# GLA decode passes, decode steps per column tile and the width of the weight rounding in a hybrid decoder layer

## The chip, the cores and the metric

The kernel runs on one core of a Trainium2 chip. The metric is the device time of one execution in microseconds; the median of three runs of the kernel before is 847.57 us.

## What is computed

One layer of a hybrid recurrent decoder, for a prompt of 256 tokens and for 8 sequences that decode one token each, 264 columns in all. A combined projection feeds an mLSTM branch and a gated linear attention (GLA) branch. Both keep a state per head; for a decoding sequence the GLA part is

```python
def _gla_chunk(q, k, v, loga, S):
    ...
    o = jnp.einsum('bhtd,bhde->bhte', q * jnp.exp(bc), S) + jnp.einsum('bhts,bhse->bhte', a, v)
    ...
    S_new = jnp.exp(last[:, :, 0, :])[..., None] * S + jnp.einsum('bhsd,bhse->bhde', k * jnp.exp(last - bc), v)
```

With one token this is S_new = a * S + k v and o = q S_new, for 8 sequences, 4 heads and a state of 128 x 256. The mLSTM decode has the same form with a state of 256 x 256. Each branch is normed per head, gated and projected; sigmoid gates merge the branches, an output projection and a LayerNorm follow.

## The kernel before

All large projections run as 128 column tiles of 128 output columns (`units()` lists them; a 129th, small one holds gate columns). A tile takes 16 blocks of contraction rows, and for each block three products of 128 x 128 weights with 264 columns: high half of the weights with the high half of the activations (L225), high with low (L226) and low with high (L230). The halves are made on the chip: `load_raw` brings 8 blocks (512 KB) by one transfer, `cast_piece` takes 4 blocks, 512 columns wide, rounds them on ScalarE to the high half (L204) and subtracts on VectorE for the low half (L206). Four raw buffers and nine pieces of each half let this run ahead of TensorE; `LA` says how many pieces are asked for ahead in the program.

In program order a loop goes over the column tiles: ask for pieces, issue the 48 products, take the result from PSUM (`e_qk`, `e_v`, `e_plain`, `e_raw`, `e_pab`, `e_out`), then call `pump(budget)`. The rest of the layer is written as generators that yield a cost after each step: gates, mLSTM prompt (`g_a_prompt`), mLSTM decode (`g_a_decode`), GLA prompt (`g_gla_prompt`), GLA decode (`g_gla_decode`), the two norms (`g_a_norm`, `g_b_norm`). `pump` takes one step of every live generator, decode ones last, as long as the budget of the tile (4.0) is above zero. TensorE's order is the program's order; the other engines are ordered by a scheduler from priorities (the rounding has the highest, prompt and norm steps the next, decode steps none). The queue that loads (SP), POOL's and each compute engine's run strictly in their order.

The tiles come in this order: q and k of the mLSTM (tiles 0 to 15), the small one (16), its v (17 to 24), q, k, v of GLA (25 to 40), output gates of both branches (41 to 64), merge gates (65 to 96, `gr`), branch projections (97 to 112), output projection (113 to 128).

`g_gla_decode` (from L759) works on 8 chunks `sch` of 4 sequences, two per head. For a head three rows `ga`, `gk`, `gq` are flattened by a small transfer and spread over the partitions by POOL (`flatten_bcast`, L493). A chunk is multiplied by `ga` in one VectorE pass of 1024 (L784). Then each sequence and half takes an update `sch = gk * v + sch` (L788) and a dot product with `gq` that accumulates into one column (L790), each 128 wide:

```python
V.tensor_tensor(out=c, in0=c, in1=ab[:, b0:b0 + 4].unsqueeze(2).to_broadcast([128, 4, 2, 128]), op=ALU.mult)
...
V.scalar_tensor_tensor(out=cc, in0=kb[:, b, :], scalar=bvd[:, 2 * h + e, b:b + 1],
                       in1=cc, op0=ALU.mult, op1=ALU.add)
V.scalar_tensor_tensor(out=scr2[:, 0:128], in0=cc, scalar=1.0, in1=qb[:, b, :], op0=ALU.mult,
                       op1=ALU.mult, accum_out=oT.t(2 * h + e)[:, L + b:L + b + 1])
```

It yields after every two sequences (a step: 16 in all), and POOL's queue stores the finished chunk (L794). `g_b_norm` squares each head of `oT` on ScalarE (`nsq`, L803), sums on VectorE (`ns`, L805) and averages over partitions on TensorE (L810).

Of the kernel before, what the change touches and what calls it, by code (L numbers as in the profile page):

```python
# [21 lines left out]
L = 256  # L22
NB = 8
# [62 lines left out]
def body(ctx, tc, xT, wbig, wsmall, par, cmask, lmask, sel, rowc, gate, wgu, cT, sT, nst, cst, lnr,  # L86
# [34 lines left out]
    def t1(name, dt=F32):  # L121
        return tmp.tile([128, T], dt, tag="t1", name=name, bufs=12)
# [10 lines left out]
    cm_sb = const.tile([128, 384], F32, name="cm_sb")  # L133
# [33 lines left out]
    def load_raw():  # L167
        i = nxt["dma"]
        if i >= len(pieces):
            return  # L170
        r = wraw_p.tile([128, KR, 128], F32, tag="raw", name="raw")
        per = KR // KC
        runs = []
        for q in range(per):
            n, c, bi = pieces[i + q]
            w = 128 if bi is not None else SMALL
            raws[i + q] = r[:, q * KC:q * KC + KC, 0:w]
            if runs and runs[-1][0] == n and runs[-1][2] == c * KC:
                runs[-1][2] += KC
            else:  # L180
                runs.append([n, c * KC, c * KC + KC, q * KC, bi, w])
        for n, k0, k1, o, bi, w in runs:
            src = wbig[bi] if bi is not None else wsmall
            nc.sync.dma_start(out=r[:, o:o + k1 - k0, 0:w], in_=src[:, k0:k1, :])
        nxt["dma"] += per

    def cast_piece():
# [3 lines left out]
        n, c, bi = pieces[i]  # L191
        w = 128 if bi is not None else SMALL
        r = raws.pop(i)
        if bi is None:
            hl = whi_p.tile([128, KC, 128], F32R, tag="hi", name="hl")
            A.copy(out=hl[:, :, 0:w], in_=r)
            V.tensor_tensor(out=hl[:, :, w:2 * w], in0=r, in1=f(hl[:, :, 0:w]), op=ALU.subtract)
            his[n, c], los[n, c] = hl[:, :, 0:2 * w], None
            nxt["cast"] += 1
# [7 lines left out]
        his[n, c], los[n, c] = h, lo  # L207
        nxt["cast"] += 1
# [5 lines left out]
    def parts(n, k0, k1, rhs, base=0):  # L214
# [5 lines left out]
        for k in range(k0, k1):  # L220
            if k % KC == 0:
                yield ps[:, 0:T]
            wh = his[n, k // KC][:, k % KC, :]
# [1067 lines left out]
```

## Time and profile before

| | |
|---|---|
| runs | 846.61, 848.86, 847.57 us, median 847.57 |
| profiled execution | 848.32 us, of which 846.5 us lie between its first and last instruction |
| TensorE busy | 824.9 us, 97% |
| VectorE busy | 630.0 us, 74% |
| ScalarE busy | 470.6 us, 56% |
| GpSimd (POOL) busy | 82.7 us, 10% |
| mean granted TensorE clock | 0.994 |

TensorE's matmuls are pipelined, so a busy TensorE is not the same as one that advances at full pace; its waits and the number of its instructions in a stretch tell more. The other engines run one instruction after the other, and there the start of the next instruction is a better price than the shown length of one.

### The profile page before, as it was taken

To read this page: it belongs to the slowest core of one execution; us is meant where nothing else is said; L and a number is where in the kernel's file an instruction comes from. 1 tells how busy PE (TensorE), PEld (TensorE's weight loads), DVE (VectorE), ACT (ScalarE), POOL (GpSimd) and SP (SyncE) were. 2 spreads that over 40 slices of the span, in tenths; PEclk is the share of its full clock that TensorE was granted. 3 is DMA by queue.
4 is the path that set the end of the run, shared out by engine and by line. 5 is a ranking of instruction groups with operands and counts; after the bars stand their busy time and mean duration, and the time that the engine had idled before them with its cause. 6 is when DMAs were issued, how large, how long until landed. Compare 5 with 4: busy or idle time off the path is not lost.

```text
span 846.5 us, 17762 instructions
## 1 busy us (share of the span) xinstructions
PE 824.9 (97%) x6773; PEld 811.4 (96%) x6773; DVE 630.0 (74%) x1354; ACT 470.6 (56%) x896; POOL 82.7 (10%) x103
## 2 busy tenths in 40 slices
PE   6999999999999999999999999988999999999996
PEld 6999999999999999999999999988999999999995
DVE  6987768645586897876786799989895777767862
ACT  5755567545464565655655665353765444455643
POOL 0000000001010210110110202220300000000211
PEclk9999999999999999999999999999999999999998
DMA  8765565545666765676787656776656665576513
GB/s 318 243 213 178 161 188 167 155 149 166 209 211 214 259 198 188 210 232 213 238 284 227 193 164 215 256 244 216 216 170 224 185 182 178 179 260 206 179 51 103
DMA packets 50917, 170.21 MB, mean 201 GB/s; under 512 B 7936, under 2 KB 8880, under 8 KB 50832
## 3 DMA queue, kind: packets, MB, share of 16 engines
q1 hardware_dynamic: 46704, 154.66, 57.8%
q0 software_dynamic: 4128, 14.42, 4.5%
q8 instruction: 53, 0.87, 0.4%
q14 instruction: 32, 0.26, 0.1%
HBM read 152.36 MB, written 16.58 MB: 200 GB/s over the span
## 4 chain that ended last, share of the span: by engine, by line
PE 89%; DMA 4%; DVE 3%; issue 1%; ACT 1%; POOL 0%; SPq 0%; ACTq 0%; POOLq 0%; DVEq 0%
PE mm L225 27%; PE mm L226 27%; PE mm L230 27%; DMA raw<-wbig 1%; DVE lo L206 1%; DMA cch<-cT 1%; PE sd L467 1%; DVE sch L788 1%; DMA sch<-sT 1%; PE sd L423 1%; DMA sS<-sch 1%; PE sd L699 1%; DVE scr L790 1%; DMA ga<-rows 1%; PE sd L403 0%
## 5 line engine op out<-in xcount | busy, mean ns | idle before, releaser
L206 DVE TENSOR_TENSOR lo<-raw,hi 128x512 fp32r<-128x512 f32 x512 | 354.8, 702 | 137.8 <-ACT hi L204 132.9
L204 ACT CAST hi<-raw 128x512 fp32r<-128x512 f32 x512 | 310.2, 618 | 255.8 <-PE mm L226 207.3
L225 PE MATMUL mm<-xh,hi 128*128 128x264 f32 x1536 | 442.4, 288 | 8.1 <-ACT hi L204 7.4
L230 PE MATMUL mm<-xh,lo 128*128 128x264 f32 x1536 | 436.8, 284 | 4.7 <-DVE lo L206 4.7
L226 PE MATMUL mm<-xl,hi 128*128 128x264 f32 x1536 | 436.7, 284 | 0.0
L225 PEld LDWEIGHTS mm<-xh,hi 128*128 128x128 f32 x1536 | 290.7, 189 | 10.2 <-ACT hi L204 7.4
L230 PEld LDWEIGHTS mm<-xh,lo 128*128 128x128 f32 x1536 | 289.4, 188 | 5.7 <-DVE lo L206 5.6
L226 PEld LDWEIGHTS mm<-xl,hi 128*128 128x128 f32 x1536 | 291.0, 189 | 0.2
L225 PE MATMUL mm<-mh,hi 128*128 128x264 f32 x256 | 72.7, 284 | 0.0
L226 PE MATMUL mm<-ml,hi 128*128 128x264 f32 x256 | 72.6, 284 | 0.0
L230 PE MATMUL mm<-mh,lo 128*128 128x264 f32 x256 | 72.3, 283 | 0.0
L226 PEld LDWEIGHTS mm<-ml,hi 128*128 128x128 f32 x256 | 48.2, 188 | 0.0
L225 PEld LDWEIGHTS mm<-mh,hi 128*128 128x128 f32 x256 | 48.1, 188 | 0.0
L230 PEld LDWEIGHTS mm<-mh,lo 128*128 128x128 f32 x256 | 48.1, 188 | 0.0
L564 DVE SCALAR_TENSOR_TENSOR cch<-kb,avd,cch 128x256 f32<-128x256 f32 x64 | 33.1, 551 | 8.0 <-POOL kb L493 4.1
L551 ACT ACTIVATE cch<-cch,decb 128x256 f32<-128x256 f32 x64 | 28.9, 501 | 13.8 <-DMA cch<-cT 13.8
L226 PE MATMUL mm<-ybl,hi 128*128 128x264 f32 x128 | 36.5, 285 | 0.0
L226 PE MATMUL mm<-yal,hi 128*128 128x264 f32 x128 | 36.4, 284 | 0.0
L225 PE MATMUL mm<-yah,hi 128*128 128x264 f32 x128 | 36.4, 284 | 0.0
L230 PE MATMUL mm<-yah,lo 128*128 128x264 f32 x128 | 36.3, 283 | 0.0
L230 PE MATMUL mm<-ybh,lo 128*128 128x264 f32 x128 | 36.2, 283 | 0.0
L225 PE MATMUL mm<-ybh,hi 128*128 128x264 f32 x128 | 36.2, 283 | 0.0
(330 smaller groups left out, 865.5 us busy)
## 6 DMA issues: line engine op xcount, KB each, us to landing
raw<-wbig SPq DMA_DIRECT2D x252, 512.0 KB
cch<-cT SPq DMA_DIRECT2D x16, 512.0 KB
sC<-cch POOLq DMA_DIRECT2D x16, 512.0 KB, 4.7
sch<-sT SPq DMA_DIRECT2D x8, 512.0 KB
sS<-sch POOLq DMA_DIRECT2D x8, 512.0 KB, 6.7
xr<-xT SPq DMA_DIRECT2D x4, 528.0 KB
raw<-wbig SPq DMA_DIRECT2D x8, 256.0 KB
y<-yt SPq DMA_DIRECT2D x8, 256.0 KB
```

The costliest lines, as they stand in the source:

```text
L204: A.copy(out=h, in_=r)
L206: E.tensor_tensor(out=lo, in0=r, in1=f(h), op=ALU.subtract)
L225: PE.matmul(out, lhsT=wh, rhs=rh, start=(k == k0), stop=False)
L226: PE.matmul(out, lhsT=wh, rhs=rl, start=False, stop=small and k == k1 - 1)
L230: PE.matmul(out, lhsT=wl, rhs=rh, start=False, stop=(k == k1 - 1))
L423: PE.matmul(S[:, o:o + n], lhsT=kT.t(2 * h + d)[:, s0:s0 + 128], rhs=qT.t(2 * h + d)[:, t0:t0 + n], start=(d == 0), stop=(d == 1))
L467: PE.matmul(CN[:, 0:VC], lhsT=kw[:, s, d * 128:d * 128 + 128], rhs=vt[h // 2][:, s, h % 2, :], start=(s == 0), stop=(s == 1))
L551: A.activation(out=c[:, b, :], in_=c[:, b, :], func=AF.Copy, scale=decb[:, h, b0 + b:b0 + b + 1])
L564: V.scalar_tensor_tensor(out=c[:, b, :], in0=kb[:, b, :], scalar=avd[:, 2 * h + e, b0 + b:b0 + b + 1], in1=c[:, b, :], op0=ALU.mult, op1=A ...
L699: PE.matmul(pl[s0:s0 + m, 4 * hf + h, n0:n0 + w].rearrange("p (n s) -> p n s", s=hs), lhsT=K[:, h, hf * 128 + s0:hf * 128 + s0 + m], rhs=r ...
L788: V.scalar_tensor_tensor(out=cc, in0=kb[:, b, :], scalar=bvd[:, 2 * h + e, b:b + 1], in1=cc, op0=ALU.mult, op1=ALU.add)
L790: V.scalar_tensor_tensor(out=scr2[:, 0:128], in0=cc, scalar=1.0, in1=qb[:, b, :], op0=ALU.mult, op1=ALU.mult, accum_out=oT.t(2 * h + e)[:, ...
```

## The change

- GLA decode: for two sequences at a time ScalarE writes the four outer products `gk * v` of 128 columns into a new tile `gkv`; VectorE then makes three passes of 512 columns (times `ga`, plus `gkv`, times `gq` into `gpr`) and a reduce of 512 columns to four. The step yields 2.6.
- mLSTM decode: same instructions; its step of two sequences yields 2.1 instead of 1.4.
- `pump`: budget 2.8 instead of 4.0; after the other generators only the first live decode generator is stepped, up to twice, as long as the budget is above zero.
- Weights: from the third tile on, a piece has 8 blocks (1024 columns) and there are five buffers of each half; the first two tiles keep pieces of 4 blocks, interleaved as before.
- Room: 11 instead of 12 scratch tiles `t1`, a mask of 256 instead of 384 columns, and four small tiles of the last stage put into tags that are free by then.

```diff
-BUDGET = 4.0
+BUDGET = 2.8
+BACK_STEPS = 2
+T1_BUFS = 11
-KC = 4
-NC = KT // KC
 KR = 8
 RAW_BUFS = 4
-CAST_BUFS = 9
+CAST_BUFS = 5
+NC = KT // KR
 LA = CAST_BUFS - NC
-RA = (RAW_BUFS - 1) * KR // KC
+HU = 2
+KH = 4
...
-        h = whi_p.tile([128, KC, 128], F32R, tag="hi", name="hi")[:, :, 0:w]
-        lo = wlo_p.tile([128, KC, 128], F32R, tag="lo", name="lo")[:, :, 0:w]
+        h = whi_p.tile([128, KR, 128], F32R, tag="hi", name="hi")[:, 0:m]
+        lo = wlo_p.tile([128, KR, 128], F32R, tag="lo", name="lo")[:, 0:m]
         with tc.high_priority(offset=PRIO):
             A.copy(out=h, in_=r)
-            E = G if POOL_LO[0] <= n < POOL_LO[1] and c in POOL_C else V
-            E.tensor_tensor(out=lo, in0=r, in1=f(h), op=ALU.subtract)
+            V.tensor_tensor(out=lo, in0=r, in1=f(h), op=ALU.subtract)
...
-                if b == 1 and SPLIT_A:
-                    yield 1.4
-            yield 1.4 if SPLIT_A else 2.7
+                if b % 2:
+                    yield 2.1
...
-                V.tensor_tensor(out=c, in0=c, in1=ab[:, b0:b0 + 4].unsqueeze(2).to_broadcast([128, 4, 2, 128]), op=ALU.mult)
-                for b in range(b0, b0 + 4):
-                    for e in range(2):
-                        cc = c[:, b - b0, e, :]
-                        V.scalar_tensor_tensor(out=cc, in0=kb[:, b, :], scalar=bvd[:, 2 * h + e, b:b + 1],
-                                               in1=cc, op0=ALU.mult, op1=ALU.add)
-                        V.scalar_tensor_tensor(out=scr2[:, 0:128], in0=cc, scalar=1.0, in1=qb[:, b, :], op0=ALU.mult,
-                                               op1=ALU.mult, accum_out=oT.t(2 * h + e)[:, L + b:L + b + 1])
-                    if b % 2 == 1:
-                        yield 2.0
+                for p in (0, 2):
+                    q, cc, sh = slice(b0 + p, b0 + p + 2), c[:, p:p + 2], [128, 2, 2, 128]
+                    kv, pr = (tmp.tile(sh, F32, tag="t2", name=x, bufs=5) for x in ("gkv", "gpr"))
+                    for i in range(2):
+                        for e in range(2):
+                            A.activation(out=kv[:, i, e, :], in_=kb[:, b0 + p + i, :], func=AF.Copy,
+                                         scale=bvd[:, 2 * h + e, b0 + p + i:b0 + p + i + 1])
+                    V.tensor_tensor(out=cc, in0=cc, in1=ab[:, q].unsqueeze(2).to_broadcast(sh), op=ALU.mult)
+                    V.tensor_tensor(out=cc, in0=cc, in1=kv, op=ALU.add)
+                    V.tensor_tensor(out=pr, in0=cc, in1=qb[:, q].unsqueeze(2).to_broadcast(sh), op=ALU.mult)
+                    V.tensor_reduce(out=oT.h(h)[:, :, L + b0 + p:L + b0 + p + 2].rearrange("p e b -> p b e"), in_=pr,
+                                    axis=mybir.AxisListType.X, op=ALU.add)
+                    yield 2.6
...
-        for g in sorted(side, key=lambda g: g.__name__ in BACK):
-            if budget <= (BACK_MIN if g.__name__ in BACK else 0):
-                continue
...
+        for g in [g for g in side if g.__name__ not in BACK]:
+            if budget > 0:
+                with tc.high_priority(offset=SIDE_PRIO):
+                    budget -= step(g)
+        for _ in range(BACK_STEPS):
+            for g in [g for g in side if g.__name__ in BACK][:1]:
+                if budget > 0:
+                    budget -= step(g)
```

What this makes of the order is shown at three places (each row: line, operation, tile written and tiles read, shape, and how many in a row). Counted by the rounding passes ahead of them, the first and last GLA passes on VectorE stand at tiles 72 and 89 before, at tiles 64 and 80 now; the last mLSTM pass moves from tile 66 to tile 59; in program order the GLA decode ends with tile 86 before and with tile 75 now.

VectorE in the middle of the GLA decode, before (`lo` is the rounding, `scr` the dot products):
```order
L784 TENSOR_TENSOR sch<-sch,ga 128x1024
L206 TENSOR_TENSOR lo<-raw,hi 128x512
L788 SCALAR_TENSOR_TENSOR sch<-gk,bvd,sch 128x128 x4
L206 TENSOR_TENSOR lo<-raw,hi 128x512
L788 SCALAR_TENSOR_TENSOR sch<-gk,bvd,sch 128x128 x2
L206 TENSOR_TENSOR lo<-raw,hi 128x512
L788 SCALAR_TENSOR_TENSOR sch<-gk,bvd,sch 128x128 x2
L790 SCALAR_TENSOR_TENSOR scr,oT_5114<-sch,gq 128x128 x2
L206 TENSOR_TENSOR lo<-raw,hi 128x512
L790 SCALAR_TENSOR_TENSOR scr,oT_5114<-sch,gq 128x128 x3
```
and now, inside tiles 73 to 76:
```order
L786 TENSOR_TENSOR sch<-sch,gkv 128x512
L203 TENSOR_TENSOR lo<-raw,hi 128x1024
L787 TENSOR_TENSOR gpr<-sch,gq 128x512
L785 TENSOR_TENSOR sch<-sch,ga 128x512
L788 TENSOR_REDUCE oT_4723<-gpr 128x2x2
L786 TENSOR_TENSOR sch<-sch,gkv 128x512
L785 TENSOR_TENSOR sch<-sch,ga 128x512
L787 TENSOR_TENSOR gpr<-sch,gq 128x512
L785 TENSOR_TENSOR sch<-sch,ga 128x512
L788 TENSOR_REDUCE oT_4723<-gpr 128x2x2
L786 TENSOR_TENSOR sch<-sch,gkv 128x512
L785 TENSOR_TENSOR sch<-sch,ga 128x512
```
Twelve narrow instructions per step have become four wide ones, and two rounding passes stand where four stood.

ScalarE around the squares `nsq` of the GLA norm, before (`hi` is the rounding cast):
```order
L803 ACTIVATE nsq<-oT_5114 128x528
L585 COPY gr<-mm 128x264
L204 CAST hi<-raw 128x512 x4
L585 COPY gr<-mm 128x264
L204 CAST hi<-raw 128x512 x4
L585 COPY gr<-mm 128x264
L827 ACTIVATE gr<-gr 128x1056
L204 CAST hi<-raw 128x512
L803 ACTIVATE nsq<-oT_5292 128x528
L204 CAST hi<-raw 128x512 x3
L585 COPY gr<-mm 128x264
```
and now, with the last outer products `gkv`:
```order
L783 ACTIVATE gkv<-gk,bvd 128x128
L202 CAST hi<-raw 128x1024
L783 ACTIVATE gkv<-gk,bvd 128x128 x3
L202 CAST hi<-raw 128x1024
L580 COPY gr<-mm 128x264
L783 ACTIVATE gkv<-gk,bvd 128x128 x4
L202 CAST hi<-raw 128x1024
L800 ACTIVATE nsq<-oT_4723 128x528 x2
L800 ACTIVATE nsq<-oT_4895 128x528
L202 CAST hi<-raw 128x1024
L580 COPY gr<-mm 128x264
L800 ACTIVATE nsq<-oT_4895 128x528
```
The squares of the heads stood four or five tiles of casts apart; now three stand together behind the last outer products, and the fourth two rows later.

POOL's queue, before (`ISA` rows are the partition broadcasts, `sS` the stores of finished chunks):
```order
L794 DMA sS<-sch 128x1024
L493 ISA ga<-ga 128x1024
L493 ISA gk<-gk 128x1024
L493 ISA gq<-gq 128x1024
L794 DMA sS<-sch 128x1024 x3
L493 ISA ga<-ga 128x1024
L493 ISA gk<-gk 128x1024
L493 ISA gq<-gq 128x1024
L794 DMA sS<-sch 128x1024 x2
L493 ISA ga<-ga 128x1024
L493 ISA gk<-gk 128x1024
L493 ISA gq<-gq 128x1024
```
and now:
```order
L791 DMA sS<-sch 128x1024 x2
L489 ISA ga<-ga 128x1024
L489 ISA gk<-gk 128x1024
L489 ISA gq<-gq 128x1024
L791 DMA sS<-sch 128x1024
L489 ISA ga<-ga 128x1024
L489 ISA gk<-gk 128x1024
L489 ISA gq<-gq 128x1024
L791 DMA sS<-sch 128x1024 x2
L489 ISA ga<-ga 128x1024
L489 ISA gk<-gk 128x1024
L489 ISA gq<-gq 128x1024
```
The broadcasts of the second, third and fourth head now follow the stores of two, three and five chunks; before, of one, four and six.

## Rows read from the trace of the kernel before

**Rows 1.** Timeline of VectorE, 640 to 680 us: start us, us, engine, line, operation, tiles, [idle before]
```profile
651.07 0.69 DVE L206 TENSOR_TENSOR lo<-raw,hi 128x512 fp32r<-128x512 f32 x1 [0.41 <-ACT hi L204]
...
656.89 0.69 DVE L206 TENSOR_TENSOR lo<-raw,hi 128x512 fp32r<-128x512 f32 x1 [0.41 <-ACT hi L204]
```
**Rows 2.** Windows: us, busy of PE, PEld, DVE, ACT, POOL (instructions), granted clock, DMA share, GB/s
```profile
320.00:340.00 20.00, 18.68 (x221) 18.02 (x220) 13.67 (x25) 11.00 (x23) 0.00 (x0) 1.00 0.57 186
...
476.00:600.00 124.00, 118.58 (x950) 117.23 (x949) 117.92 (x305) 63.57 (x120) 22.83 (x21) 0.99 0.68 218
...
564.00:567.00 3.00, 1.77 (x15) 1.56 (x14) 2.90 (x6) 2.56 (x6) 0.17 (x2) 1.00 0.38 131
569.00:571.00 2.00, 1.07 (x9) 0.93 (x8) 1.93 (x10) 0.31 (x1) 0.40 (x1) 1.00 0.41 156
580.00:584.00 4.00, 1.41 (x11) 1.20 (x11) 2.58 (x4) 2.15 (x5) 0.00 (x0) 1.00 0.70 281
584.00:588.00 4.00, 4.00 (x23) 4.00 (x22) 4.00 (x17) 2.02 (x5) 0.00 (x0) 0.57 0.68 205
```
**Rows 3.** Waits of TensorE: engine, line, what was waited for, us in total, times, longest
```profile
PE mm L230 <- DVE lo L206: 4.7, 3, 2.6
```
**Rows 4.** Timeline of ScalarE, 470 to 600 us
```profile
562.44 0.65 ACT L803 ACTIVATE nsq<-oT 128x528 f32<-128x528 f32 x1 [3.35 <-DVE scr L790]
...
570.69 0.62 ACT L204 CAST hi<-raw 128x512 fp32r<-128x512 f32 x1 [2.87 <-DMA raw<-wbig]
...
579.16 0.65 ACT L803 ACTIVATE nsq<-oT 128x528 f32<-128x528 f32 x1 [5.95 <-DVE scr L790]
```
**Rows 5.** Timeline of VectorE in the GLA decode, no broadcast in flight
```profile
528.94 1.22 DVE L784 TENSOR_TENSOR sch<-sch,ga 128x1024 f32<-128x1024 f32 x1
530.08 1.28 DVE L206 TENSOR_TENSOR lo<-raw,hi 128x512 fp32r<-128x512 f32 x2
531.28 0.87 DVE L788 SCALAR_TENSOR_TENSOR sch<-gk,bvd,sch 128x128 f32<-128x128 f32 x3
532.07 0.68 DVE L206 TENSOR_TENSOR lo<-raw,hi 128x512 fp32r<-128x512 f32 x1
...
538.70 0.28 DVE L790 SCALAR_TENSOR_TENSOR scr<-sch,gq 128x128 f32<-128x128 f32 x1
...
539.02 0.29 DVE L790 SCALAR_TENSOR_TENSOR scr<-sch,gq 128x128 f32<-128x128 f32 x1
```
**Rows 6.** Groups of ScalarE by line and shape: count | busy us, mean ns of one | idle before
```profile
L204 ACT CAST hi<-raw 128x512 fp32r<-128x512 f32 x512 | 310.2, 618 | 255.8 <-PE mm L226 207.3 <-DMA raw<-wbig 24.1 <-ACT mh L211 7.9
L551 ACT ACTIVATE cch<-cch,decb 128x256 f32<-128x256 f32 x64 | 28.9, 501 | 13.8 <-DMA cch<-cT 13.8
L585 ACT COPY gr<-mm 128x264 f32<-128x264 f32 x32 | 11.9, 374 | 5.3 <-DVE sch L784 4.3 <-DVE sch L788 1.0
...
L827 ACT ACTIVATE gr<-gr 128x1056 f32<-128x1056 f32 x8 | 8.7, 1088 | 0.2
...
L929 ACT CAST lgh<-lgf 128x1024 fp32r<-128x1024 f32 x2 | 2.1, 1048 | 3.6 <-DMA lgf<-lnr 3.6
...
L710 ACT ACTIVATE gE<-gB 128x128 f32<-128x128 f32 x1 | 0.3, 307 | 0.0
```
**Rows 7.** Timeline of VectorE with a partition broadcast of POOL in flight
```profile
539.63 1.64 DVE L206 TENSOR_TENSOR lo<-raw,hi 128x512 fp32r<-128x512 f32 x1
541.19 1.39 DVE L805 TENSOR_TENSOR ns<-nsq 128x264 f32<-128x264 f32 x1
542.50 2.18 DVE L784 TENSOR_TENSOR sch<-sch,ga 128x1024 f32<-128x1024 f32 x1
...
565.84 0.43 DVE L805 TENSOR_TENSOR ns<-nsq 128x264 f32<-128x264 f32 x1
...
567.12 1.12 DVE L790 SCALAR_TENSOR_TENSOR scr<-sch,gq 128x128 f32<-128x128 f32 x1
...
568.28 1.12 DVE L790 SCALAR_TENSOR_TENSOR scr<-sch,gq 128x128 f32<-128x128 f32 x1
```

More of the change, by code (lines that the diff above doesn't have):

```diff
@@ L155, in f @@
         return ap.bitcast(F32)
-    pieces = []
-    idx = 0
+    pieces = [(u, k, KH, u) for k in range(0, KT, KH) for u in range(HU)]
+    idx = HU
     for n, (kind, j) in enumerate(UN):
+        if n < HU:
+            continue
         bi = None if kind == "small" else idx
         idx += kind != "small"
-        pieces += [(n, c, bi) for c in range(NC)]
-    pieces[0:2 * NC] = [pieces[u * NC + c] for c in range(NC) for u in range(2)]
+        pieces += [(n, k, KR, bi) for k in range(0, KT, KR)]
+    last = {n: i for i, (n, k, w, bi) in enumerate(pieces)}
     raws, his, los = {}, {}, {}
@@ L171, in load_raw @@
         r = wraw_p.tile([128, KR, 128], F32, tag="raw", name="raw")
[L172 to L175, printed above, removed]
+        o = 0
+        while i < len(pieces) and o + pieces[i][2] <= KR:
+            n, k, m, bi = pieces[i]
             w = 128 if bi is not None else SMALL
[L177 to L182, printed above, removed]
-            src = wbig[bi] if bi is not None else wsmall
-            nc.sync.dma_start(out=r[:, o:o + k1 - k0, 0:w], in_=src[:, k0:k1, :])
-        nxt["dma"] += per
+            src = wbig[bi] if bi is not None else wsmall
+            raws[i] = r[:, o:o + m, 0:w]
+            nc.sync.dma_start(out=raws[i], in_=src[:, k:k + m, :])
+            o += m
+            i += 1
+        nxt["dma"] = i
     def cast_piece():
@@ L190, in cast_piece @@
             load_raw()
-        n, c, bi = pieces[i]
-        w = 128 if bi is not None else SMALL
+        n, k, m, bi = pieces[i]
+        nxt["cast"] += 1
         r = raws.pop(i)
+        h = whi_p.tile([128, KR, 128], F32R, tag="hi", name="hi")[:, 0:m]
         if bi is None:
[L195 to L199, printed above, removed]
+            w = SMALL
+            A.copy(out=h[:, :, 0:w], in_=r)
+            V.tensor_tensor(out=h[:, :, w:2 * w], in0=r, in1=f(h[:, :, 0:w]), op=ALU.subtract)
+            for q in range(m):
+                his[n, k + q] = h[:, q, 0:2 * w]
             return
-        h = whi_p.tile([128, KC, 128], F32R, tag="hi", name="hi")[:, :, 0:w]
-        lo = wlo_p.tile([128, KC, 128], F32R, tag="lo", name="lo")[:, :, 0:w]
+        lo = wlo_p.tile([128, KR, 128], F32R, tag="lo", name="lo")[:, 0:m]
         with tc.high_priority(offset=PRIO):
             A.copy(out=h, in_=r)
-            E = G if POOL_LO[0] <= n < POOL_LO[1] and c in POOL_C else V
-            E.tensor_tensor(out=lo, in0=r, in1=f(h), op=ALU.subtract)
-        his[n, c], los[n, c] = h, lo
-        nxt["cast"] += 1
+            V.tensor_tensor(out=lo, in0=r, in1=f(h), op=ALU.subtract)
+        for q in range(m):
+            his[n, k + q], los[n, k + q] = h[:, q], lo[:, q]
     def split(hi, lo, src):
@@ L773, in g_gla_decode @@
         load(0)
-        scr2 = tmp.tile([128, 256], F32, tag="t1", name="scr", bufs=12)
         yield 0.1
@@ L1016, in ln_final @@
             emit(1, g)
-        sm_ = one.tile([128, 4, NB], F32, tag="lsm", name="lsm")
+        sm_ = one.tile([128, 4, NB], F32, tag="qkd", name="lsm")
         dd, d2, sv = sm_[:, 0], sm_[:, 1], sm_[:, 2]
@@ L1026, in ln_final @@
         zd = ln["zd"]
-        td = one.tile([128, 16, NB], F32, tag="td", name="td")
+        td = one.tile([128, 16, NB], F32, tag="co", name="td")
         sh = [128, 16, NB]
@@ L1084, in body @@
         V.memset(one_c, 1.0)
-        first = [parts(u, 0, 16, x_rhs) for u in range(2)]
+        first = [parts(u, 0, 16, x_rhs) for u in range(HU)]
         head = {}
@@ L1103, in body @@
             st['n'] = n
-            while nxt["cast"] < NC * (n + 1) + LA and nxt["cast"] < len(pieces):
+            while nxt["cast"] < min(last[n] + 1 + LA, len(pieces)):
                 cast_piece()
-                while nxt["dma"] < min(nxt["cast"] + RA, len(pieces)):
+                while nxt["dma"] < min(nxt["cast"] + RAW_BUFS - 1, len(pieces)):
                     load_raw()
```

90 lines of the change are left out of this document (40 added, 50 removed).

## The prediction

> **What bounds the kernel now.** I read first the windows of the engines' busy time, then the waits of TensorE, then the timelines around those waits. In the steady part TensorE sets the pace: the reader is to see two rounding passes of VectorE, four pieces apart, that is one column tile, which each wait for a cast that in turn waits for TensorE to release a buffer. They are 656.89 - 651.07 = 5.82 us apart [rows 1]. No vector or scalar work that hides under this pace is worth anything. So only the places count where TensorE does wait. They lie in one stretch, 476 to 600 us, where VectorE is busy 117.92 of 124 us [rows 2]. That is the GLA decode together with the mLSTM norm. TensorE misses 3.00 - 1.77 = 1.23 us at 564, 2.00 - 1.07 = 0.93 us at 569 and 4.00 - 1.41 = 2.59 us at 580 [rows 2]. The sum, 4.75 us, is what the table of waits puts down to the low halves of the weights, 4.7 us in 3 waits [rows 3]. [...] Together 6.45 us. One wait of 20.00 - 18.68 = 1.32 us lies earlier, at 329 us [rows 2], in the mLSTM decode. **The pool to be won is 7.8 us, under 1% of the time.**
>
> The timeline of ScalarE says how the waits come about. A square of the GLA norm stands in its queue ahead of three or four rounding casts, and waits 3.35 and 5.95 us for the last VectorE pass of its head; once a cast waits 2.87 us for its weights [rows 4]. VectorE was late, and the rounding behind it used up its lead.
>
> **The change part by part.** Starts of neighbours in the queue, not durations, give the price of a VectorE pass when it is saturated: 1024 wide with two inputs 530.08 - 528.94 = 1.14 us, 512 wide (531.28 - 530.08) / 2 = 0.60 us, a 128-wide update (532.07 - 531.28) / 3 = 0.26 us, a 128-wide dot product with its accumulator read 539.02 - 538.70 = 0.32 us [rows 5].
>
> GLA decode, per step of two sequences: before, half a 1024-wide pass, four updates, four dot products, 0.57 + 1.05 + 1.28 = 2.90 us. After, three 512-wide passes at 0.60 and one reduce. No row shows a reduce. Nearest below is the 0.26 us update (four times less data), nearest above the 1.14 us pass (twice the data); I take the 512-wide 0.60 us. So 2.40 us a step, and 16 x 0.50 = 8.0 us less on VectorE.
>
> Rounding: a tile's four passes of 0.60 become two of 1.14, 0.12 us less. On ScalarE four casts of 0.618 us become two; the nearest row is 1.048 us for a 1024-wide cast [rows 6], 0.38 us less. Outside the GLA stretch both gains lie beside TensorE's 5.82 us and cost or earn nothing; if that cover went, it would be because VectorE or ScalarE filled a tile, which outside this stretch they don't. The lead shrinks a little: five buffers leave four pieces of half a tile, 11.6 us, less one wide cast (1.05) and one wide pass (1.14), 9.5 us; before it was 11.6 - 0.6 - 0.6 = 10.4 us.
>
> The outer products: 64 new instructions of 128 columns on ScalarE. Nearest rows: 0.307 us for 128 columns with a constant scale, 0.501 us for 256 columns with a scale per row [rows 6]; I take 0.34 us, nearer to the row of the same width. With two steps in a tile ScalarE holds 2 x 1.05 + 8 x 0.34 + 0.374 for the copy out of PSUM + a quarter of the 1.088 us gate, 5.5 of 5.82 us [rows 6]. It is covered, but thinly.
>
> The order. GLA decode starts eight tiles earlier on VectorE and ends nine earlier, so the norm of its branch is done well ahead of the projection that needs it; that in itself earns nothing, as nothing waited there for long. The twelve partition broadcasts stay. Each holds VectorE up: with them in flight a rounding pass takes 1.64 us, a sum 1.39, a wide pass 2.18, each 0.96 us over its usual time (0.68, 0.43, 1.22), 2.9 us for this head; the last head shows two dot products of 1.12 us, 0.84 over their 0.28, 1.7 us [rows 5, 7]. Mean 2.3 us a head. In the changed order VectorE's work is not even: between the rounding of tile 72 and that of tile 76 stand 25 two-input passes of 512, 8 reduces and 8 wide rounding passes. That is 33 x 0.60 + 8 x 1.14 = 28.9 us. POOL's queue lets the broadcasts of the second, third and fourth head go only after two, three and five chunks are done, all of it in or just ahead of these tiles: 3 x 2.3 = 6.9 us. VectorE needs 35.8 us, TensorE takes 4 x 5.82 = 23.3 us, the excess is 12.5 us against a lead of 9.5 us: **TensorE will wait about 3.0 us, near tiles 75 to 77.** Bounds: reduces at 0.26 us and 1.7 us a head give 28.9 - 2.7 + 5.1 - 23.3 - 9.5, below zero, so none; reduces at 1.14 us and 2.9 us a head give 28.9 + 4.3 + 8.7 - 23.3 - 9.5 = 9.1 us, and 1.7 us of clock on top.
>
> [...] The row: back to back, 512-wide passes start 0.60 us apart although each is shown as 0.68 to 0.69 us long [rows 5]. [...]
>
> The mLSTM decode takes up to two steps per tile where it took one, and none in tiles with a long prompt step. It ends seven tiles earlier. Its instructions are the same; VectorE and ScalarE have room there. I price it at zero. The wait of 1.32 us at 329 us may go or come twice: bounds -1.3 and +1.3. The SP queue carries the same loads; raw weights stand behind state loads as before, with three pieces loaded ahead. The smaller mask, the shared small tiles and 11 instead of 12 scratch buffers change no instruction's length; the scratch buffers are covered by VectorE's lead, and if not, cost what that lead loses. The head and the last 17 us keep their order.
>
> **Sum.** The profiled execution took 848.32 us; the median of the runs is 847.57, 0.75 lower. 848.32 - 6.45 (the three waits and the clock) + 3.0 (the new wait) = 844.9; less 0.75, and with a little for the ScalarE waits that no longer stand one by one between the casts on one side and a chance of clock loss on the other, which I let cancel: **844.5 us**.
>
> **Rivals.**
> A. No wait is left in the decode. For it: the squares of the norm now stand together behind the last reduce instead of one per head among the casts [rows 4]; VectorE's work falls by 8.0 us and more. Against it: the crowded tiles. 848.32 - 6.45 - 0.75 = 841.1 us, 839.8 if the early wait goes too.
> B. The wait returns in its old size: passes follow each other at their shown length, 0.68 and 1.22 us, or broadcasts hold each head up by 2.9 us. The wait is then 3.0 + 3.3 or 3.0 + 1.8 us: 848.32 - 6.45 + 4.8 - 0.75 = 845.9 us, or 847.4 us, with the clock up to 849.1. [...] For it: the crowding stands in the order. No difference that a measurement tells.
> C. ScalarE's queue becomes the bound, and it is slower. The first outer product of a head waits for the second of three broadcasts and for a scratch buffer that a reduce must free, and the next cast stands behind it. A wait like the 3.35 us of the squares [rows 4] at two of the heads whose lead is already used up adds 6.7 us, with 1.7 us for the clock: 848.32 - 6.45 + 3.0 + 6.7 + 1.7 - 0.75 = 852.5 us. It decides once such a wait exceeds the half tile, 2.9 us, that one piece covers. For it: ScalarE at 5.5 of 5.82 us; at 0.40 us per outer product it is over. Against it: in the changed order the outer products of a step stand a step or more ahead of the pass that uses them.
> That the change doesn't do what it says is not open: the order shows the passes, the outer products and the wide rounding.
>
> **How the numbers follow.** Forecast case, 842 to 846.5 us: 0.42. A: 0.20. B beyond that: 0.22. C: 0.16. A measurement of this kernel tells 0.3%, 2.5 us, from no change, so faster means below 845.0. A and three quarters of the forecast case lie there, 0.50; C and the worst of B are above 850.1, 0.18; the rest, 0.32, is no change. The range takes the lower end of A and the upper end of B with the nearer part of C: 839.5 to 850.5 us.
>
> **What would show it.** In the profile after: no wait of TensorE near the places of rows 2 but one or two, 2 to 5 us together, while VectorE works on the third and fourth head; two-input passes of 512 at about 0.69 us shown, a reduce near 0.6; outer products near 0.34 us; ScalarE's waits for VectorE shorter than 3 us. Wrong would be: waits in the mLSTM decode, reduces beyond 1 us, ScalarE waiting at the outer products with casts behind them, or a clock of 0.5 in more than one place.

## The result and the profile after

The changed kernel takes 853.16 us in the median of four runs (851.88 to 854.27), the kernel before 848.22 us beside it (846.61 to 848.88): ratio 1.0067, 95% interval 1.0052 to 1.0083. It is slower by about 5.7 us. The forecast was 844.5 us with a range up to 850.5; the time lies above it, nearest to rival C's 852.5. The profiled execution took 851.88 us, the fastest of the four, with a span of 850.1 us.

Busy time of the engines, first section of the page:
```profile
PE 827.8 (97%) x6773; PEld 813.9 (96%) x6773; DVE 604.8 (71%) x964; ACT 453.8 (53%) x706; POOL 87.8 (10%) x103
```
VectorE and ScalarE do have less to do than before, 604.8 instead of 630.0 us and 453.8 instead of 470.6. The loss is in TensorE's waits, the counterpart of [rows 3]. Each row names the engine, tile and line that waited, what it waited for, us in total, times, and the longest:
```profile
PE mm L222 <- ACT hi L202: 6.4, 1, 6.4
PE mm L226 <- DVE lo L203: 4.6, 1, 4.6
PE sd L807 <- DVE ns L802: 2.5, 2, 1.4
PE sd L637 <- DVE ns L630: 1.3, 1, 1.3
```
The first row is the start of the kernel. Three waits for low halves have become one of 4.6 us, and two places are new: the matmuls that average the squares of the two norms, L807 (GLA) and L637 (mLSTM). Windows of 1 us around the long wait (us, TensorE busy and instructions, granted clock, DMA share, GB/s), the counterpart of the last two of [rows 2]:
```profile
518.00:519.00 1.00, 0.51 (x5) 1.00 0.00 0
...
521.00:522.00 1.00, 0.00 (x0) 0.90 0.57 234
522.00:523.00 1.00, 0.00 (x0) 0.50 0.00 0
523.00:524.00 1.00, 0.93 (x4) 0.50 0.03 4
...
527.00:528.00 1.00, 1.00 (x6) 0.50 0.82 274
528.00:529.00 1.00, 1.00 (x8) 0.69 1.11 250
```
TensorE stands still from 518.5 to 523.1 us; the granted clock, 1.00 until 521, falls to 0.50 while it stands, stays there until 528, and is 0.69 in the window behind and 1.00 from 529 on. Busy time times what is missing of the clock, summed from 523 to 529 us, gives 2.8 us more. Behind it TensorE waits twice at the GLA norm:
```profile
538.60 1.57 PE L807 MATMUL sd<-ns,inv 128*128 128x264 f32 x6 [1.40 <-DVE ns L802]
541.26 0.71 PE L807 MATMUL sd<-ns,inv 128*128 128x264 f32 x2 [1.09 <-DVE ns L802]
```
Why the low halves were late stands in VectorE's timeline:
```profile
481.56 1.22 DVE L203 TENSOR_TENSOR lo<-raw,hi 128x1024 fp32r<-128x1024 f32 x1 [0.81 <-ACT hi L202]
483.98 3.10 DVE L785 TENSOR_TENSOR sch<-sch,ga 128x512 f32<-128x512 f32 x2 [1.19 <-POOL ga L489]
487.00 1.21 DVE L203 TENSOR_TENSOR lo<-raw,hi 128x1024 fp32r<-128x1024 f32 x1
...
500.44 0.67 DVE L788 TENSOR_REDUCE oT<-gpr 128x4 f32<-128x512 f32 x1
501.04 0.68 DVE L786 TENSOR_TENSOR sch<-sch,gkv 128x512 f32<-128x512 f32 x1
501.64 0.68 DVE L785 TENSOR_TENSOR sch<-sch,ga 128x512 f32<-128x512 f32 x1
...
511.76 1.58 DVE L203 TENSOR_TENSOR lo<-raw,hi 128x1024 fp32r<-128x1024 f32 x1
513.27 1.64 DVE L786 TENSOR_TENSOR sch<-sch,gkv 128x512 f32<-128x512 f32 x1
514.84 1.65 DVE L785 TENSOR_TENSOR sch<-sch,ga 128x512 f32<-128x512 f32 x1
516.40 0.68 DVE L787 TENSOR_TENSOR gpr<-sch,gq 128x512 f32<-128x512 f32 x1
...
521.20 0.68 DVE L786 TENSOR_TENSOR sch<-sch,gkv 128x512 f32<-128x512 f32 x1
521.80 1.21 DVE L203 TENSOR_TENSOR lo<-raw,hi 128x1024 fp32r<-128x1024 f32 x1
```
Between the rounding passes at 511.76 and 521.80 us stand eleven GLA passes in a row, the first two held up by broadcasts to 1.57 us from start to start. For ten microseconds no low half is begun, where TensorE uses up a piece every 2.9 (it came to two in a row at 492.24 and 495.14 us). The first three rows show that VectorE had fallen back before: it stood idle 1.19 us for the spread row `ga` of the second head, and the two passes behind it took 487.00 - 483.98 = 3.02 us under the broadcasts where two take 1.20. ScalarE at the same time:
```profile
514.54 1.28 ACT L783 ACTIVATE gkv<-gk,bvd 128x128 f32<-128x128 f32 x4 [4.43 <-POOL gk L489]
515.73 1.03 ACT L202 CAST hi<-raw 128x1024 fp32r<-128x1024 f32 x1
516.66 0.36 ACT L580 COPY gr<-mm 128x264 f32<-128x264 f32 x1
516.93 1.05 ACT L202 CAST hi<-raw 128x1024 fp32r<-128x1024 f32 x1
```
The outer products of the last head waited 4.43 us for their spread row, with the casts behind them: the very picture of rival C. So two theories were open. **Crowding:** the new pump presses two GLA steps into a tile and VectorE has no room for them. **ScalarE's queue:** the outer products hold up the casts. A third is the **wide rounding**, which comes in coarser pieces.

### The profile page after: what moved, and what is told of

The parts are those of the page before. It is cut to its first block, busy times and chain, and to the rows that moved or that the text cites. A ratio compares the mean times of both kernels' runs of the same rounds, so it can differ in the third digit from the quotient of the medians.

```text
span 850.1 us, 16785 instructions
## 1 busy us (share of the span) xinstructions
PE 827.8 (97%) x6773; PEld 813.9 (96%) x6773; DVE 604.8 (71%) x964; ACT 453.8 (53%) x706; POOL 87.8 (10%) x103
## 5 line engine op out<-in xcount | busy, mean ns | idle before, releaser
L222 PE MATMUL mm<-xh,hi 128*128 128x264 f32 x1552 | 447.3, 289 | 6.4 <-ACT hi L202 6.4
L226 PE MATMUL mm<-xh,lo 128*128 128x264 f32 x1536 | 437.7, 285 | 4.6 <-DVE lo L203 4.6
L223 PE MATMUL mm<-xl,hi 128*128 128x264 f32 x1552 | 441.7, 285 | 0.0
L203 DVE TENSOR_TENSOR lo<-raw,hi 128x1024 fp32r<-128x1024 f32 (+1 forms) x260 | 316.1, 1218 | 155.5 <-ACT hi L202 153.3
L202 ACT CAST hi<-raw 128x1024 fp32r<-128x1024 f32 (+1 forms) x260 | 268.1, 1034 | 295.5 <-PE mm L223 269.2
L222 PEld LDWEIGHTS mm<-xh,hi 128*128 128x128 f32 x1552 | 294.4, 190 | 8.5 <-ACT hi L202 6.4
L226 PEld LDWEIGHTS mm<-xh,lo 128*128 128x128 f32 x1536 | 290.5, 189 | 5.1 <-DVE lo L203 5.1
L223 PEld LDWEIGHTS mm<-xl,hi 128*128 128x128 f32 x1552 | 294.5, 190 | 0.5 <-DVE xl L209 0.3
L226 PE MATMUL mm<-mh,lo 128*128 128x264 f32 x256 | 72.7, 284 | 0.0
L226 PEld LDWEIGHTS mm<-mh,lo 128*128 128x128 f32 x256 | 48.1, 188 | 0.0
L843 POOL TENSOR_TENSOR xt<-xh,xl 128x264 f32<-128x264 f32 x16 | 17.0, 1077 | 207.2 <-DVE zt L854 188.4
L226 PE MATMUL mm<-ybh,lo 128*128 128x264 f32 x128 | 36.3, 284 | 0.0
L226 PE MATMUL mm<-yah,lo 128*128 128x264 f32 x128 | 36.2, 283 | 0.0
```

The source lines that it names most:

```text
L203: V.tensor_tensor(out=lo, in0=r, in1=f(h), op=ALU.subtract)
L222: PE.matmul(out, lhsT=wh, rhs=rh, start=(k == k0), stop=False)
L223: PE.matmul(out, lhsT=wh, rhs=rl, start=False, stop=small and k == k1 - 1)
L226: PE.matmul(out, lhsT=los[n, k], rhs=rh, start=False, stop=(k == k1 - 1))
L843: G.tensor_tensor(out=xt, in0=f(x_hi[j // 4][:, j % 4, :]), in1=f(x_lo[j // 4][:, j % 4, :]), op=ALU.add)
```

## The experiments

Each was timed beside the kernel before, and its ratio is to that kernel. Medians of runs that were not timed together can differ by 1.4 us for that reason alone, as those of the kernel before do (846.78 to 848.22). "Steps" says how many GLA decode steps the pump lets into a tile: before, one, starting late; the change, up to two, starting at tile 64; "one, early" is the change with its second step withheld. Waits are TensorE's after the start of the kernel, in the one execution of each that was profiled.

| run | GLA passes | steps | rounding | median us | ratio to before (95%) | waits, us |
|---|---|---|---|---|---|---|
| before | narrow | one, late | 512 | | 1 | 4.7 low halves, 1.3 prompt, 0.7 at 511 us |
| e11_wide_rounding | narrow | one, late | 1024 | 845.14 | 0.9965 (0.9953 to 0.9977) | 2.8 low half, 0.4 |
| e4_body | wide | one, late | 512 | 843.76 | 0.9955 (0.9938 to 0.9971) | 1.6 prompt, 1.2 mLSTM norm |
| e2_pump | wide | one, late | 1024 | 841.86 | 0.9929 (0.9912 to 0.9946) | 1.4 mLSTM norm, 1.3 in three |
| e1_narrow | narrow | two | 1024 | 855.49 | 1.0095 (1.0079 to 1.0111) | 4.0 high half, 2.1 low halves, 2.1 and 1.5 norms |
| e3_512 | wide | two | 512 | 853.99 | 1.0077 (1.0057 to 1.0096) | 3.1 low half, 3.0 and 1.4 norms |
| the change | wide | two | 1024 | 853.16 | 1.0067 (1.0052 to 1.0083) | 4.6 low half, 2.5 and 1.3 norms |
| e10_narrow_one | narrow | one, early | 1024 | 841.44 | 0.9932 (0.9917 to 0.9946) | 1.5 mLSTM norm |
| e12_512_one | wide | one, early | 512 | 842.18 | 0.9937 (0.9924 to 0.9950) | 2.1 mLSTM norm |
| e6_one | wide | one, early | 1024 | 841.08 | 0.9924 (0.9910 to 0.9939) | 1.4 mLSTM norm |

**e4_body**, the kernel before with the new GLA passes alone (the part of the diff under `g_gla_decode`, step still 2.0).

> The kernel before with the new GLA decode passes alone (old pump, old rounding of 512). Theory 1, crowding: the loss of the change comes from the tiles into which its pump presses the GLA passes; in the old order they stand 5 to 7 to a tile instead of up to 12, so the three waits of 4.7 us shrink to at most 1.5 us and the 1.7 us of clock goes: 843 to 845 us, faster than before by 0.4% to 0.6%. Theory 2, ScalarE's queue: outer products that wait for the spread rows hold the casts behind them wherever they stand, so waits of 4 us or more stay: 848 to 851 us.

It gained 3.8 us (0.45%), and the waits at low halves are gone: as crowding expected. No loss comes from the passes.

**e2_pump**, the change with the old pump.
```diff
-BUDGET = 2.8
+BUDGET = 4.0
...
-                    yield 2.1
+                    yield 1.4
...
-                    yield 2.6
+                    yield 2.0
...
-        for _ in range(BACK_STEPS):
+        for g in sorted(side, key=lambda g: g.__name__ in BACK):
```


> The changed kernel with the old pump (budget 4.0, one step of each generator, yields 1.4 and 2.0). It differs from the run with the new passes alone by the rounding of 1024 columns and the smaller rooms. Theory 1, crowding: within 1.5 us of that run, 843 to 846 us. Theory 3, the wide rounding: pieces of half a tile come in coarser steps and cost lead, 2 to 4 us slower than that run, 847 us or more.

841.86 us: the other two parts together win 6.0 us, and all of the change's loss sits in the pump. The wide rounding costs nothing; this is 1.9 us faster than e4_body, better than any theory had it, though the two intervals overlap.

**e3_512**, the change with 512-wide pieces for all tiles.
```diff
-CAST_BUFS = 5
-NC = KT // KR
+CAST_BUFS = 9
+NC = KT // 4
...
-        pieces += [(n, k, KR, bi) for k in range(0, KT, KR)]
+        pieces += [(n, k, KH, bi) for k in range(0, KT, KH)]
```


> The changed kernel with pieces of 512 columns and nine buffers again for all tiles. Theory 1, crowding: the lead grows by about 0.9 us, the order of the GLA passes stays nearly as it is (12 in one tile), so 851 to 853 us. Theory 3, the wide rounding: the wait and the clock loss behind it go, 845 to 848 us.

853.99 us, a little more than crowding expected; the loss is unchanged, and the third theory falls. The low-half wait is 3.1 instead of 4.6 us, but the wait at the GLA norm is 3.0 instead of 2.5, and the clock behind the 3.1 us takes another 2.9.

**e6_one**, one number: with the step at 2.9 and the budget at 2.8 a second step never fits.
```diff
-                    yield 2.6
+                    yield 2.9
```


> The changed kernel with the GLA step yielding 2.9 instead of 2.6, so that the budget of 2.8 lets at most one step into a tile: 2 to 5 GLA passes a tile in the order where there were up to 12. Theory 1, crowding: VectorE is no longer saturated, the 4.6 us wait and the clock loss of some 3 us behind it go, and with them the wait of 2.5 us at the GLA norm's matmuls: 842.5 to 845 us. Theory 2, ScalarE's queue: the outer products of each head still wait for the second spread row with casts behind them, so a wait of 3 us or more remains: 848 us or more.

841.08 us, 12 us below the change and 1.4 below what crowding expected. TensorE's waits:
```profile
PE mm L222 <- ACT hi L202: 7.2, 1, 7.2
PE sd L637 <- DVE ns L630: 1.4, 1, 1.4
```
ScalarE's outer products still wait 6.4 us for spread rows in this run, 3.8 us at the longest, and it costs TensorE nothing. Such waits in ScalarE's queue are not the cause on their own. What differs is where VectorE's work lies. Windows of VectorE (us, busy and instructions, clock, DMA share, GB/s) of the change:
```profile
500.00:520.00 20.00, 19.97 (x26) 1.00 0.60 206
520.00:540.00 20.00, 19.21 (x27) 0.83 0.77 265
540.00:560.00 20.00, 18.80 (x17) 1.00 0.44 131
560.00:580.00 20.00, 13.96 (x14) 1.00 0.66 210
580.00:600.00 20.00, 8.57 (x7) 1.00 0.58 182
```
and of e6_one:
```profile
500.00:520.00 20.00, 16.33 (x20) 1.00 0.79 264
520.00:540.00 20.00, 15.96 (x18) 1.00 0.69 226
540.00:560.00 20.00, 18.49 (x24) 1.00 0.76 247
560.00:580.00 20.00, 16.63 (x16) 1.00 0.57 188
580.00:600.00 20.00, 15.02 (x15) 1.00 0.66 207
```
The sums are 80.5 and 82.4 us; the change puts them early and leaves VectorE with little to do from 560 us on.

**e1_narrow**, the change with the old passes.
```diff
...
-                    V.tensor_tensor(out=cc, in0=cc, in1=kv, op=ALU.add)
...
+                        V.scalar_tensor_tensor(out=cc, in0=kb[:, b, :], scalar=bvd[:, 2 * h + e, b:b + 1],
+                                               in1=cc, op0=ALU.mult, op1=ALU.add)
...
```


> The changed kernel with the old GLA decode passes (a 1024-wide pass, updates and dot products of 128) in the new order. Theory 1, crowding: the same two steps a tile, each 0.5 us longer on VectorE, in the tiles that decide, 5 or 6 steps more work than they can hide: 3 us or more on top of the changed kernel, 856 to 862 us; the order alone costs 9 us or more against before. Theory 2, ScalarE's queue: without outer products no cast stands behind a wait for the spread rows, so faster than the changed kernel, 847 to 851 us.

855.49 us. Without a single outer product the loss is no smaller, so outer products that wait for spread rows are not needed for it; the 2.3 us above the change are somewhat less than crowding expected, and the intervals of the two just overlap. ScalarE's queue has a part in this run all the same, in another way. TensorE's longest wait here, 4.0 us, is for a cast, and that cast stood behind a square of the GLA norm which waited for VectorE:
```profile
521.82 0.64 ACT L798 ACTIVATE nsq<-oT 128x528 f32<-128x528 f32 x1 [12.72 <-DVE scr L785]
```
VectorE is busy throughout this wait, and with one step a tile (e10_narrow_one below) TensorE has no such wait. Against e11_wide_rounding, which has the same passes and rounding, the pump costs 1.0095 - 0.9965 = 1.3%, 11 us.

**e5_ahead**, rows of the next head loaded and spread half a head earlier.
```diff
...
+                if bh and h + 1 < H:
+                    ahead = spread(h + 1)
```


> The changed kernel with the rows of each head loaded and spread half a head earlier, ahead of the store of the last chunk on POOL's queue; the hold-up of VectorE by the spreads stays. In its order the most GLA passes in a tile are 9 instead of 12, mostly 6. Theory 1, crowding: six passes, two rounding passes and 2.3 us of hold-up for every head still fill a tile of 5.82 us (3.6 + 2.3 us and 2.3 us in every second or third tile), so some wait stays but most of the 4.6 us and the clock loss go: 845 to 849 us. Theory 2, ScalarE's queue: once no outer product waits for a spread row nothing is left to lose, as with one step a tile: 841 to 844 us.

851.96 us, ratio 1.0059 (1.0044 to 1.0073), outside what either theory expected. No low half is waited for any more, though one is done only 0.4 us before TensorE comes to it; but the norms are:
```profile
PE sd L637 <- DVE ns L630: 4.2, 1, 4.2
PE sd L814 <- DVE ns L809: 2.8, 1, 2.8
```
The loss moved. VectorE's timeline shows the first of the two: the spreads of the second head now fall into the mLSTM norm.
```profile
437.69 0.68 DVE L793 TENSOR_TENSOR sch<-sch,gkv 128x512 f32<-128x512 f32 x1
438.29 1.65 DVE L792 TENSOR_TENSOR sch<-sch,ga 128x512 f32<-128x512 f32 x1
439.85 1.65 DVE L794 TENSOR_TENSOR gpr<-sch,gq 128x512 f32<-128x512 f32 x1
441.42 1.65 DVE L792 TENSOR_TENSOR sch<-sch,ga 128x512 f32<-128x512 f32 x1
442.99 1.21 DVE L203 TENSOR_TENSOR lo<-raw,hi 128x1024 fp32r<-128x1024 f32 x1
444.12 0.76 DVE L630 TENSOR_TENSOR ns<-nsq 128x264 f32<-128x264 f32 x2
```
The same passes in the change, with no broadcast in flight:
```profile
437.62 0.68 DVE L786 TENSOR_TENSOR sch<-sch,gkv 128x512 f32<-128x512 f32 x1
438.22 0.68 DVE L785 TENSOR_TENSOR sch<-sch,ga 128x512 f32<-128x512 f32 x1
...
441.17 0.76 DVE L630 TENSOR_TENSOR ns<-nsq 128x264 f32<-128x264 f32 x2
```
Three passes of 1.57 instead of 0.60 us make 2.9 us; the sums `ns` start 444.12 - 441.17 = 2.95 us later, and TensorE's wait grows from 1.3 to 4.2.

**e7_norm**, two empty steps ahead of the GLA norm's matmuls.
```diff
             if h % 2:
                 yield 1.2
+        yield 1.2
+        yield 1.2
```


> The changed kernel with two empty steps ahead of the GLA norm's four matmuls, so that they stand two tiles later in TensorE's order. Theory 1 with in-order TensorE: the 2.5 us that it waits at them go, the rest stays: 850 to 851.5 us. Rival: VectorE's backlog is what costs, the same wait turns up at the next low halves: 852.5 to 854 us.

848.68 us, ratio 1.0017 (1.0008 to 1.0026), 0.5% or 4.5 us below the change, where 2.5 us were expected. Between the two profiled executions it is 851.88 - 848.84 = 3.0 us, about what the waits explain; the rest lies in the executions that were not profiled. The wait at the norm is gone and none takes its place:
```profile
PE mm L226 <- DVE lo L203: 4.3, 1, 4.3
PE sd L637 <- DVE ns L630: 1.4, 1, 1.4
```

**e8_rows**, no spreads for the second to fourth head, which take the rows of the first instead of their own.
```diff
-            ab, kb, qb = (t4([128, NB, 128], "g" + x) for x in "akq")
-            for i, x in enumerate((ab, kb, qb)):
-                flatten_bcast(x, rows[32 * i + 8 * h:32 * i + 8 * h + 8, :])
+            if h == 0:
+                ab, kb, qb = (t4([128, NB, 128], "g" + x) for x in "akq")
+                for i, x in enumerate((ab, kb, qb)):
+                    flatten_bcast(x, rows[32 * i:32 * i + 8, :])
```


> The changed kernel without the spreads of the second to fourth head: all heads use the rows of the first. That leaves out nine small transfers and nine broadcasts. In its order there are 6 GLA passes a tile. Theory 1, crowding with the hold-up of VectorE: 6 x 0.60 + 2.28 = 5.9 us a tile against 5.82, the lead lasts; no wait at low halves: 842 to 846 us, and 3 us or more below the run with the rows spread earlier if the hold-up of 2.3 us a head is what fills it. Theory 2, ScalarE's queue: within 1 us of the run with the rows spread earlier, since both have no outer product that waits.

842.03 us, ratio 0.9938 (0.9925 to 0.9952). Two steps a tile are affordable once the broadcasts are gone: 6 passes a tile, no low half late, only 1.6 and 1.4 us at the norms. Against e5_ahead, where the outer products hardly wait either but the broadcasts are there, it is 10 us faster. So it is the spreads, and not outer products that wait for them, for which two steps a tile leave no room. How much of that is their hold-up of VectorE is not shown, since leaving them out also evens the order: between two rounding passes stand at most 4 GLA passes here, 8 in e5_ahead and 11 in the change.

**e10_narrow_one**, the old passes with one step a tile (e1_narrow with 2.9 for 2.6).

> The changed kernel with the old narrow GLA passes and one step a tile (yield 2.9). Theory 1, crowding: a step of 2.9 us, two rounding passes of 1.14 us and 2.3 us of hold-up at each head make 5.2 us a tile, 7.5 in four of sixteen; the lead of 9.5 us covers it, the wait and the clock loss go: 841 to 845 us, at least 11 us below the same passes with two steps a tile, so the order and not the passes decides. Rival: the passes decide, 0.5 us more a step on VectorE keeps it full: 847 us or more.

841.44 us, 14 us below e1_narrow. Spread by one step, narrow and wide passes take the same time to within the intervals.

**e11_wide_rounding**, the wide rounding alone (e2_pump with the old passes).

> The wide rounding and the smaller rooms without the other two parts: old GLA passes, old pump. In its order 12 to 16 narrow passes stand in a tile, as before. Theory 1, crowding: the three waits of 4.7 us and the clock loss stay about as they are, VectorE saves only 0.12 us a tile: 845 to 848 us. Theory 3 turned round, that the wide rounding is a gain of its own (old order and new passes: 843.8 us with 512, 841.9 us with 1024): 842 to 845 us.

845.14 us, a gain of 3.0 us, between the two expectations: in the profiled execution one wait of 2.8 us at a low half stays of three, as do 2.9 us of clock behind it. That execution, 846.88 us, is the slowest of its ten; the fastest took 842.22 us with a mean granted clock of 0.998 instead of 0.993, so the clock loss at least is not in each. Which property of the wide pieces removes the other two was not tried.

**e12_512_one**, 512-wide pieces with one step a tile.

> The changed kernel with one GLA step a tile (yield 2.9) and pieces of 512 columns for all tiles. Theory 1, crowding: with at most 6 GLA passes in a tile the width does not matter, within 1 us of the same with 1024, 840 to 842.5 us. Theory 3, turned round as above: 2 us or so slower than that, 842.5 to 844 us.

842.18 us against 841.08: the width decides little once the steps are spread, as crowding expected.

**e9_best**, e6_one with the mLSTM norm's second matmuls a tile later.
```diff
             if h % 2:
                 yield 2.4
+        yield 2.8
         for h in range(H):
             vp = side_ps()[:, 0:T]
```


> The changed kernel with one GLA step a tile (yield 2.9) and an empty step of 2.8 ahead of the second four matmuls of the mLSTM norm, so that they stand a tile later. If in-order TensorE loses its last 1.4 us at these matmuls and nothing waits behind, 1.0 to 1.6 us below the run with one step a tile, 839.5 to 840.5 us, the fastest of all. Rival: VectorE's backlog turns the wait up at the next matmuls or low halves: the same as that run, 840.7 to 841.5 us.

839.94 us, ratio 0.9916 (0.9899 to 0.9933), the lowest of all, though by the intervals not told apart from e6_one: 7 us below the kernel before and 13 below the change. The empty step uses up the whole budget of its tile, so the GLA steps behind it also move by one tile. One TensorE wait is left, the start:
```profile
PE mm L222 <- ACT hi L202: 7.5, 1, 7.5
```
though outer products wait longer than ever, 6.5 us once:
```profile
ACT gkv L784 <- POOL gk L489: 9.8, 3, 6.5
```

## Why the prediction was wrong

**What held.** The bound, and the pool of 7.8 us: with everything spread 7 us are won. The prices: reduces and 512-wide passes start 0.60 us apart (500.44, 501.04, 501.64), four outer products take 515.73 - 514.54 = 1.19 us, 0.30 each against 0.34, a wide cast is shown as 1.03 to 1.06. The broadcasts of the third and of the fourth head hold VectorE up by 2.3 us each (for the fourth 0.37 + 0.97 + 0.97, at the starts 511.76, 513.27, 514.84, 516.40). The three old waits went, with their clock: the 6.45 us of the sum are the 4.75 us of waiting and the 4.00 x (1 - 0.57) = 1.7 us that went behind the longest of them [rows 2], where windows of 1 us show a granted clock of 0.67, 0.50, 0.50 and 0.63 from 584 to 588 us. And the new wait lies where it was put: between its end at 523.07 us and the first product of tile 97 at 646.2 us stand 320 products with low halves (L226), 16 to a tile. That is 20 tiles, so TensorE waited for the first low half of tile 77.

**What failed is the term of 3.0 us for the new wait.** It was the excess of one four-tile stretch of VectorE over a lead, and nothing else was attached to the crowding. Measured, the two steps a tile cost 4.6 us at the low half, 2.8 of clock and 2.5 at the GLA norm: 9.9 us. Three steps in the term were wrong:
- The lead was taken as whole. It was, half a tile before the stretch: the low half begun at 481.56 us was done at 482.78, and TensorE came to it at 492.24, 9.5 us later. The next one, the first of tile 73, was begun only at 487.00 us, after the idle time for `ga` and the two held-up passes; it was done at 488.21 and TensorE came to it at 495.14. So 6.9 us of lead were left. From 487.00 to 521.80 us VectorE then needed 34.8 us (35 GLA passes, 8 rounding passes, the broadcasts of two heads; the forecast had 35.8 us for 33 passes and three heads), an excess of 34.8 - 23.3 = 11.5 us, and 11.5 - 6.9 = 4.6 us is the wait. The excess came out 1.0 us below the forecast, the lead 2.6 us below it.
- The clock was set off against a gain in ScalarE's waits ("which I let cancel"). The wait brought 2.8 us of it along. Wait and clock, 7.4 us, still lie inside the bounds that the term had, 9.1 and 1.7 us; but these bounds give 848.32 - 6.45 + 10.8 - 0.75 = 851.9 us, and the range was closed at 850.5.
- The GLA norm was priced at nothing, as "nothing waited there for long". Its matmuls stand in TensorE's queue as written in the program, right behind the decode steps that keep VectorE full, and moving the decode forward moved them with it. e7_norm, which only moves these matmuls, removes the 2.5 us.

Beside it stands the wait of 1.3 us at the mLSTM norm, also priced at nothing. It does not come from the second step: e4_body and e2_pump show 1.2 and 1.4 us there with the old pump, e6_one and e10_narrow_one 1.4 and 1.5 with one step a tile. What makes it stays open; e9_best removes it.

Eleven GLA passes in one piece add nothing to this sum, since they lie inside the stretch. Whether the first low half of tile 77 could have gone ahead of some of them is another matter: in e8_rows, where no rows are waited for, the order is even, six passes a tile. Why the scheduler makes one lump of them otherwise was not tried.

The mLSTM decode, priced at zero with a bound of -1.3, gained 1.3 us: the wait that stood at 329 us is gone. A smaller wait went too, 124.00 - 118.58 - 4.75 = 0.7 us of the stretch from 476 to 600 us [rows 2], which the sum had left aside. The start took 0.9 us longer, by the first matmul behind the gate tile, before
```profile
L288 PE MATMUL sd<-hl,par_sb x2: 384/386/387, 111.7 to 112.0; 96*80 96x264 f32 x2
```
and after
```profile
L284 PE MATMUL sd<-hl,par_sb x2: 383/385/387, 112.7 to 112.9; 96*80 96x264 f32 x2
```
The account: forecast for the profiled execution 844.9, + 1.6 (wait) + 2.8 (clock) + 3.8 (the two norms) - 1.3 - 0.7 (old waits) + 0.9 (start) = 852.0 us; it took 851.88. The median lies another 1.3 above this one. The 0.9 us of the start need be no effect of the change: the executions of e8_rows and e11_wide_rounding, alike with the change in the program up to there, differ by 1.0 us at the same place (112.17 and 113.17 us).

**Rival C** gave 852.5 us and came within 0.7. That is luck, as it expected two waits of 3.35 us in ScalarE's queue to reach TensorE, and none of the change's waits came about so. Casts did stand behind an outer product for 4.4 us at one head. But its point of decision, a wait beyond the 2.9 us that one piece covers, is refuted: 3.8 us in e6_one and 6.5 in e9_best cost TensorE nothing, since the lead covered them. In e6_one the last low half ahead of that wait was done 8.7 us before TensorE came to it, the next one (begun at 536.57 us) still 3.5 us before; in e9_best these were 8.1 and 5.4 us, and between 425 and 600 us no lead is shorter than 3.2 us in either. In the change it was down to 0.3 us at the low half begun at 505.24 us, behind ten GLA passes, and 2.1 us at that of 511.76. Rival A's 841.1 us is what the change gives with one step a tile.

**Rival B** gave 845.9 or 847.4 us, and neither of its conditions was met. Passes of 512 columns do not follow each other at their shown length: in the saturated stretch they start 0.60 us apart and are shown as 0.67 to 0.68 us long. And the broadcasts of the third and of the fourth head held VectorE up by 2.3 us each, not by 2.9.

## What to carry to other kernels

Background work under a saturated engine is not priced by its sum but by the fullest stretch, with everything that falls into it, and by the lead that is left where that stretch begins, not by the full one. Here 0.3 in a yield, which decides whether one step or two go into a tile, is worth 12 us, and the rewritten passes next to nothing once they are spread. Before moving such work forward, look at what stands behind it in the in-order queue of the bounding engine (here eight small matmuls of a norm), and give that a tile or two of room. An engine that waits for several microseconds can be harmless (6.5 us in e9_best); look first at the lead behind it, and then judge the wait.

## What the runs showed of the hardware

In these traces a stand-still of TensorE cost more than its length in eight cases, but not in proportion. Clock lost behind one (busy time times what is missing of the clock, in us): 1.7 us behind 2.6 us (before), 2.9 behind 2.8 (e11_wide_rounding), 1.6 behind 2.8 and 1.7 behind 4.2 (e5_ahead), 2.9 behind 3.1 and none behind 3.0 (both e3_512), 3.0 behind 4.0 with one of 0.9 close after it (e1_narrow), 2.7 behind 4.3 (e7_norm), 2.8 behind 4.6 (the change); none behind the 2.1 us at the GLA norm in e1_narrow, the 1.40 us there in the change, or the 1.23 and 0.93 us before, where the windows show 1.00.

The start differs between executions by as much as a small change is worth. The first matmul behind the gate tile stands between 111.55 us (e12_512_one) and 113.17 us (e11_wide_rounding), in kernels whose first two tiles come in the same pieces. In the change TensorE's matmuls start 0.22 us apart from 7.9 until 13.2 us and 0.12 apart from there, where each is shown as 0.28 us long; before, the slow ones ended at 10.7. The windows show the granted clock as 1.00 from 7 to 15 us all the same; that TensorE ran at half pace until 13.2 us is read from the pitch, since 0.22 us is also the pitch at 524 us, where they show 0.50.

Three two-input passes of 512 columns in a row, at 438.29, 439.85 and 441.42 us in e5_ahead, stand beside partition broadcasts shown from 437.89, 439.39 and 440.95 us, and each starts its successor 1.56 or 1.57 us later instead of 0.60, 0.97 us each. Two at 513.27 and 514.84 us in the change cost the same.

VectorE, ScalarE and POOL took their work in the order listed ahead of the prediction: in the trace of the change the twelve VectorE rows start at 495.20 to 504.64 us, the ScalarE rows around the squares at 527.60 to 539.83 and POOL's at 468.37 to 514.37, each in its place.
